# One group fewer by seven products, state's copy on ScalarE, and the y products in a portion of their own

## The chip, the cores and the metric

The kernel runs on one core of a Trainium2 chip. TensorE (PE) multiplies, VectorE (DVE), ScalarE (ACT) and GpSimd (POOL) do the element-wise work, and transfers are issued from queues, most of the weights' from SyncE's (SP). The metric is the device time of one execution in microseconds (us); before the change the median of three runs is 1458.86 us, from 1458.23 to 1462.82.

## What is computed

One decoder layer on 256 tokens of width 2048, in float32. A normalised input is multiplied by one wide matrix, whose columns are split into the gate z, the inputs x, B, C and dt of a state-space part (SSD), and q, k, v of an attention part:

```python
def hybrid_mixer(u, w_in, ...):
    z, xbc, dt_raw, q, k, v = jnp.split(u @ w_in, IN_SPLITS, axis=-1)
    xbc = silu(causal_depthwise_conv(xbc, conv_w, conv_b))
    xs, bm, cm = jnp.split(xbc, ...)          # 8 groups of 4 heads of 64
    y = ssd_chunked(xh, softplus(dt_raw + dt_bias), -exp(a_log), bm, cm) + d_skip * xh
    yg = y * silu(z)
    yg = yg * rsqrt(mean(yg * yg, axis=-1) + EPS)      # by group
    y_att = dilated_window_attention(...)              # three dilations, combined
    return concat([yg * ssm_norm_w, y_att]) @ w_out

h = x + rmsnorm(hybrid_mixer(rmsnorm(x), ...))
out = h + rmsnorm(relu(rmsnorm(h) @ w_up) ** 2 @ w_down)
```

`ssd_chunked` works on two chunks of 128 tokens. Inside a chunk y is (C Bᵀ, masked and multiplied by decays) times x·dt. The second chunk also gets C times the state that the first leaves, times a decay. That second term is `yo` below, and the first chunk's state is `st`.

## The kernel before

**Products.** The 256 tokens are two tiles of 128, the 2048 rows of a weight 16 tiles of 128. Weights come in blocks of two row tiles and 512 columns (`raw`, four buffers, SP's queue), and a block is one k step. Since TensorE multiplies in a reduced form of fp32, every tile is split in two: ScalarE rounds it to `hi` (line 147) and VectorE takes the rest, `lo` (line 148), with five buffers of each. The buffer of a `hi` is free again once TensorE has finished the block of five steps before. Each product is then hi·hi + hi·lo + lo·hi: three matmuls of 512 columns where tokens are the rows of the result (`row_tile`, lines 328 to 330). For x, B and C the features are the rows, and one matmul of 512 columns (line 475, the two parts of the tokens side by side) and one of 256 (line 478) do it.

**Seven products.** z, v, out, up and down are made in units of two column blocks (`unit`). `order` is the order of their k steps, and a group k that is named in `by_seven` is multiplied in Strassen's manner (`seven`): for two column blocks and two row tiles, seven products of three matmuls (lines 411 to 413) in place of eight. It pays for that with sums of weights (`pair`, added up by transfers on POOL's queue, and three adds on VectorE, line 252), with four weight tiles to split instead of two, and with sums of the tokens' blocks (`sums_of_acts`, lines 368 to 371 and a split), which are made once for each k and kept in `sums_of`. z has two units, at about 85 to 127 us and 235 to 277 us, and both use the same sums. At the first group by seven of a unit all waiting work is drained.

**Head groups.** `ssd_group` is a generator for one of the eight groups of four heads, and what lies between two of its `yield`s is a portion. After each conversion block of x two of them are appended to `waiting`, and `pump` runs one portion of each in turn as the k steps of the next products go by, so the instructions of a pair of groups stand interleaved with matmuls of x, B, C. The four pairs lie at about 128 to 162, 176 to 208, 279 to 311 and 320 to 346 us. A group's work in order: C·B and the transpose of B (lines 793, 794), which ScalarE copies to `bn` (799); transposes of x (804), copied to `xs` (806); x·dt on VectorE (809); on POOL `xdd` (811) and the skip term (813); the decays `bc` on ScalarE (820, 821; exp needs a table load when SiLU came before) and VectorE (822); the state's matmul (825) and copy (827); state times C (829), times decay `yo` (831), added by POOL (833); the y products (837), the gate and norm (840 to 855); the last transposes (857), split into `sh` (149) and `sl` (150) for the output product.

All these small results go through two banks of PSUM (`psm`, tiles named ps). A matmul into a ps tile waits until the engine that reads the tile before in that bank has done so. The order in which instructions stand on an engine is set by the scheduler from the program's order and its priorities; each engine runs its own in that order.

The conversion block (`conv`, lines 744 to 753) and the additions of the two halves of a feature product (`added`, lines 498 and 499) run beside it on the same engines.

Of the kernel before, what the change touches and what calls it, by code (L numbers as in the profile page):

```python
# [13 lines left out]
AF = mybir.ActivationFunctionType  # L14
# [3 lines left out]
S = 256  # L18
# [59 lines left out]
def hymba_layer(ctx: ExitStack, tc: tile.TileContext, x, norm_mix_pre, w_in, conv_w, conv_b, dt_bias, a_log,  # L78
                d_skip, ssm_norm_w, w_out, norm_mix_post, norm_mlp_pre, w_up, w_down, norm_mlp_post,
                consts, out):  # L80
    nc = tc.nc
# [53 lines left out]
    def psmall():  # L135
        return psm.tile([P, NB], F32, name="ps")

    def rsqrt_mean(dst, sums, n):

        m = cp.tile(list(sums.shape), F32, name="rm", bufs=2)  # L140
        nc.vector.tensor_scalar(m, sums, 1.0 / n, EPS, op0=ALU.mult, op1=ALU.add)
        nc.gpsimd.tensor_tensor(dst, m, half[:, :sums.shape[1]], op=ALU.pow)

    def split(hi, lo, src, scale=None):

        if scale is None:
            return (nc.scalar.activation(hi, src, AF.Copy),  # L147
                    nc.vector.tensor_tensor(lo, src, hi.bitcast(F32), op=ALU.subtract))  # L148
        return (nc.scalar.activation(hi, src, AF.Copy, scale=scale),
                nc.vector.scalar_tensor_tensor(lo, src, scale, hi.bitcast(F32), op0=ALU.mult, op1=ALU.subtract))  # L150
# [105 lines left out]
    w_z, w_v, w_ups, w_downs = w_in[:, COL_Z:], w_in[:, COL_V:], [w_up[:, hf * 4096:] for hf in range(2)], [w_down, w_down[4096:]]  # L256
    orders = {}

    def order_of(ks, by_seven):
        return [(k, k in by_seven) for k in ks]  # L260

    def plan(name, src, n, order, by_seven):

        orders[name, n] = order_of(order, by_seven)
        pairs.extend((src, n * NB, k) for k in order if k in by_seven)
# [157 lines left out]
            nc.vector.tensor_tensor(b[0], more[1], u, op=ALU.add)  # L423
            nc.vector.tensor_tensor(b[1], more[3], b[0], op=ALU.add)

    plan("z", w_z, 0, (0, 2, 4, 6, 1, 3, 5), (1, 3, 5))
    plan("z", w_z, 2, (0, 2, 1, 4, 3, 6, 5), (1, 3, 5))
    for n in (0, 2):
        plan("v", w_v, n, range(7), V_SEVENS)
# [353 lines left out]
    def ssd_group(sp, g, bT, cT, xT, z):  # L783

        hs = slice(HPG * g, HPG * (g + 1))
        bc = sp.tile([P, HPG, S], F32, name="bc")
        nc.scalar.dma_start(bc, acs_d[hs].partition_broadcast(P))
        yield

        p = psmall()  # L790
        for c in range(NT):
            cs = slice(c * P, (c + 1) * P)
            nc.tensor.matmul(p[:, cs], bT[:, cs], cT[:, cs], start=True, stop=True)
        nc.tensor.transpose(p[:, S:S + P], bT[:, 0:P], ident)
        cbm = sp.tile([P, NT, P], F32, name="cbm")
        nc.vector.tensor_tensor(cbm, p[:, :S].rearrange("p (c i) -> p c i", c=NT),
                                triu[:, None, :].to_broadcast([P, NT, P]), op=ALU.mult)
        bn = sp.tile([P, P], F32, name="bn")
        nc.scalar.activation(bn, p[:, S:S + P], AF.Copy)

        p = psmall().rearrange("p (c f) -> p c f", c=NT)
        for c in range(NT):
            for f in range(2):
                nc.tensor.transpose(p[:, c, f * P:(f + 1) * P], xT[:, f, c * P:(c + 1) * P], ident)
        xs = sp.tile([P, NT, HPG, HD], F32, name="xs")
        nc.scalar.activation(xs.rearrange("p c r d -> p c (r d)"), p, AF.Copy)
        xdt = sp.tile([P, NT, HPG, HD], F32, name="xdt")
        for c in range(NT):
            nc.vector.tensor_tensor(xdt[:, c], xs[:, c], dt[:, c, hs, None].to_broadcast([P, HPG, HD]), op=ALU.mult)
        xdd = sp.tile([P, HPG, HD], F32, name="xdd")  # L810
        nc.gpsimd.tensor_tensor(xdd, xdt[:, 0], toend[:, hs, None].to_broadcast([P, HPG, HD]), op=ALU.mult)
        for c in range(NT):
            nc.gpsimd.tensor_tensor(xs[:, c], xs[:, c], skip_b[:, hs, None].to_broadcast([P, HPG, HD]), op=ALU.mult)
        yield

        for c in range(NT):
            m = bc[:, :, c * P:(c + 1) * P]
            for r in range(HPG):
                h = HPG * g + r
                nc.scalar.activation(m[:, r], m[:, r], AF.Relu, scale=-1.0, bias=acs[:, c, h:h + 1])  # L820
            nc.scalar.activation(m, m, AF.Exp, scale=-1.0)
            nc.vector.tensor_tensor(m, m, cbm[:, c, None, :].to_broadcast([P, HPG, P]), op=ALU.mult)

        p = psmall()
        nc.tensor.matmul(p[:, :S], bn, xdd.rearrange("p r d -> p (r d)"), start=True, stop=True)
        st = sp.tile([P, HPG * HD], F32, name="st")
        nc.vector.tensor_copy(st, p[:, :S])
        yield
        nc.tensor.matmul(p[:, S:], cT[:, P:], st, start=True, stop=True)
        yo = sp.tile([P, HPG, HD], F32, name="yo")  # L830
        nc.vector.tensor_tensor(yo, p[:, S:].rearrange("p (r d) -> p r d", r=HPG),
                                eacs[:, hs, None].to_broadcast([P, HPG, HD]), op=ALU.mult)
        nc.gpsimd.tensor_tensor(xs[:, 1], xs[:, 1], yo, op=ALU.add)
        p = psmall().rearrange("p (c r d) -> p c r d", c=NT, r=HPG)
        for c in range(NT):
            for r in range(HPG):
                nc.tensor.matmul(p[:, c, r], bc[:, r, c * P:(c + 1) * P], xdt[:, c, r], start=True, stop=True)  # L837

        yg = sp.tile([P, NT, HPG * HD], F32, name="yg")
        nc.vector.tensor_tensor(yg, p.rearrange("p c r d -> p c (r d)"), xs.rearrange("p c r d -> p c (r d)"),  # L840
                                op=ALU.add)
        nc.vector.tensor_tensor(yg, yg, z, op=ALU.mult)
        gs = sp.tile([P, NT], F32, name="gs")
        for c in range(NT):
            junk = sp.tile([P, HPG * HD], BF16, name="gj")
            nc.scalar.activation(junk, yg[:, c], AF.Square, accum_out=gs[:, c:c + 1])
        gr = sp.tile([P, NT], F32, name="gr")
        rsqrt_mean(gr, gs, HPG * HD)
        for c in range(NT):
            nc.vector.tensor_scalar(yg[:, c], yg[:, c], gr[:, c:c + 1], None, op0=ALU.mult)  # L850
        yield
        yield
        yield
        p = psmall().rearrange("p (f s) -> p f s", f=2)
        for f in range(2):
            for c in range(NT):
                nc.tensor.transpose(p[:, f, c * P:(c + 1) * P], yg[:, c, f * P:(f + 1) * P], ident)
        with tc.high_priority(offset=200):
            for f in range(2):
                k = 2 * g + f  # L860
                split(sh[:, k], sl[:, k], p[:, f], w_ssm[:, k:k + 1])
# [3 lines left out]
    for hb in range(2):  # L865
        bT = conv_block(COL_B + hb * NB, 16 + 4 * hb, first if hb == 0 else None)
        if hb == 0:
            waiting.append(steps())
        cT = conv_block(COL_C + hb * NB, 24 + 4 * hb)
        for xb in (2 * hb, 2 * hb + 1):  # L870
            xT = conv_block(COL_X + xb * NB, 4 * xb)
            if xb % 2 == 0:
                zs += gates(xb)
            for j in range(2):
                g = 2 * xb + j
                waiting.append(ssd_group(sp, g, bT[:, g % 4], cT[:, g % 4], xT[:, 2 * j:2 * j + 2],
                                         zs[xb][:, :, j * 256:(j + 1) * 256]))
# [623 lines left out]
```

## Time and profile before

| | |
|---|---|
| median of 3 runs | 1458.86 us (1458.23 to 1462.82) |
| profiled execution | 1459.04 us |
| its span in the trace | 1457.3 us |
| granted TensorE clock, mean | 0.999 |
| TensorE busy | 1446.1 us |
| VectorE busy | 1281.2 us |
| ScalarE busy | 939.1 us |
| GpSimd busy | 150.3 us |
| largest queue of transfers | 272.37 MB, 58.6% of 16 engines' span |

The span is what the instructions' records cover; 1.7 us of the execution lie around it. Busy time is the union of an engine's instructions, which on TensorE overlap: a row's "mean ns" is the length of one matmul, not what the next waits. In a row of the timeline the first number is the start, the second how long the row (one instruction or several of a kind) lasts; out<-in are the tiles by their names in the program; a bracket at the end is the engine's idle time before it, with what ended it. Line numbers are those of the kernel before.

### The profile page before, as it was taken

The numbers are of one execution on the slowest core, as the hardware profiler recorded it, in microseconds if no ns is written. First come the engines' busy times: TensorE is split into PE (matmuls) and PEld (weight loads), VectorE is DVE, ScalarE is ACT, GpSimd is POOL, SyncE is SP. The second block draws the span as 40 slices with busy tenths as digits, with TensorE's granted clock in tenths as the row PEclk, the third lists the DMA queues.
The fourth block names the chain that finished last, engine by engine and source line by source line (L and its number), as shares of the span: only waits on it lengthen the run. The fifth ranks groups of instructions, "written<-read, shape, count | busy, mean of one in ns | idle before, by whom it ended". The sixth has DMA issues, their size and how long they took to land.

```text
span 1457.3 us, 20381 instructions
## 1 busy us (share of the span) xinstructions
PE 1446.1 (99%) x7099; PEld 1219.4 (84%) x7099; DVE 1281.2 (88%) x1843; ACT 939.1 (64%) x1346; POOL 150.3 (10%) x226
## 2 busy tenths in 40 slices
PE   9999999999999999999999999999999999999998
PEld 8888888888888888888888888888888888888886
DVE  7799898888997686689878999999889999999997
ACT  7577779566666565556657677656464776765664
POOL 0202120121010010010100011011111111101000
PEclk9999999999999999999999999999999999999999
DMA  8978556856675486688876798678888888788854
GB/s 271 279 204 235 177 175 185 247 174 202 186 220 174 130 238 202 194 261 253 270 224 213 207 318 240 196 223 255 249 238 275 257 245 247 208 281 258 260 181 160
DMA packets 170201, 328.27 MB, mean 225 GB/s; under 512 B 15617, under 2 KB 18545, under 8 KB 170097
## 3 DMA queue, kind: packets, MB, share of 16 engines
q1 hardware_dynamic: 144592, 272.37, 58.6%
q0 software_dynamic: 17632, 40.91, 14.0%
q10 hardware_dynamic: 7872, 13.68, 2.7%
q8 instruction: 56, 0.92, 0.2%
q14 instruction: 49, 0.39, 0.1%
HBM read 322.67 MB, written 45.12 MB: 252 GB/s over the span
## 4 chain that ended last, share of the span: by engine, by line
PE 95%; DVE 3%; ACT 1%; issue 1%; POOL 0%; ACTq 0%; DVEq 0%
PE acc L475 13%; PE acc L328 11%; PE acc L330 11%; PE acc L329 11%; PE acc L478 7%; PE acc L412 6%; PE acc L413 6%; PE acc L411 6%; PE ps L330 3%; PE ps L328 3%; PE ps L329 3%; PE ps L412 3%; PE ps L413 2%; PE ps L411 2%; DVE lo L148 1%; PE ps L837 1%
## 5 line engine op out<-in xcount | busy, mean ns | idle before, releaser
L148 DVE TENSOR_TENSOR lo<-raw,hi 128x1024 fp32r<-128x1024 f32 (+1 forms) x392 | 476.8, 1221 | 86.0 <-ACT hi L147 82.7
L147 ACT ACTIVATE hi<-raw 128x1024 fp32r<-128x1024 f32 (+1 forms) x392 | 409.7, 1050 | 209.0 <-PE acc L330 70.6
L475 PE MATMUL acc<-ua,hi 128*128 128x512 f32 x600 | 162.5, 400 | 0.0
L475 PEld LDWEIGHTS acc<-ua,hi 128*128 128x128 f32 x600 | 105.5, 189 | 16.4
L147 ACT ACTIVATE hi<-e 128x1024 fp32r<-128x1024 f32 x64 | 68.1, 1064 | 69.1 <-DVE e L252 64.2
L478 PEld LDWEIGHTS acc<-ua,lo 128*128 128x128 f32 x600 | 88.2, 190 | 10.0
L478 PE MATMUL acc<-ua,lo 128*128 128x256 f32 x600 | 91.5, 282 | 0.0
L328 PE MATMUL acc<-hi,sh 128*128 128x512 f32 x224 | 88.4, 395 | 0.0
L330 PE MATMUL acc<-hi,sl 128*128 128x512 f32 x224 | 87.3, 390 | 0.0
L329 PE MATMUL acc<-lo,sh 128*128 128x512 f32 x224 | 87.2, 389 | 0.0
L328 PE MATMUL acc<-hi,ua 128*128 128x512 f32 x216 | 85.5, 396 | 0.0
L329 PE MATMUL acc<-lo,ua 128*128 128x512 f32 x216 | 84.2, 390 | 0.0
L330 PE MATMUL acc<-hi,ua 128*128 128x512 f32 x216 | 84.2, 390 | 0.0
L148 DVE TENSOR_TENSOR lo<-e,hi 128x1024 fp32r<-128x1024 f32 x64 | 78.0, 1219 | 0.0
L475 PE MATMUL acc<-uc,hi 128*128 128x512 f32 x240 | 69.9, 402 | 0.0
L412 PE MATMUL acc<-lo,ah 128*128 128x512 f32 x174 | 67.8, 390 | 0.0
L411 PE MATMUL acc<-hi,ah 128*128 128x512 f32 x174 | 67.8, 389 | 0.0
L413 PE MATMUL acc<-hi,al 128*128 128x512 f32 x174 | 67.7, 389 | 0.0
L148 DVE TENSOR_TENSOR lo<-ha,hi 128x1024 fp32r<-128x1024 f32 x43 | 52.3, 1221 | 5.9 <-ACT hi L147 5.7
L147 ACT ACTIVATE hi<-ha 128x1024 fp32r<-128x1024 f32 x43 | 45.1, 1056 | 16.2 <-PE acc L330 9.5
L147 ACT ACTIVATE hi<-r 128x512 fp32r<-128x512 f32 x64 | 40.1, 627 | 18.3 <-PE acc L330 7.0
L330 PE MATMUL acc<-hi,al 128*128 128x512 f32 x128 | 49.8, 389 | 0.0
(544 smaller groups left out, 3612.7 us busy)
## 6 DMA issues: line engine op xcount, KB each, us to landing
raw<-in_w_in_dram SPq DMA_DIRECT2D x161, 512.0 KB, 4.5
raw<-in_w_down_dram SPq DMA_DIRECT2D x72, 512.0 KB, 5.2
raw<-in_w_up_dram SPq DMA_DIRECT2D x65, 512.0 KB, 4.7
raw<-in_w_out_dram SPq DMA_DIRECT2D x38, 512.0 KB, 5.1
pair<-in_w_up_dram POOLq DMA_DIRECT2D x56, 256.0 KB, 5.0
raw<-pair SPq DMA_DIRECT2D x52, 256.0 KB, 4.2
pair<-in_w_down_dram POOLq DMA_DIRECT2D x50, 256.0 KB, 6.2
ha<-in_w_up_dram SPq DMA_DIRECT2D x20, 512.0 KB, 4.9
```

Source lines behind the costliest of these rows:

```text
L147: return (nc.scalar.activation(hi, src, AF.Copy), nc.vector.tensor_tensor(lo, src, hi.bitcast(F32), op=ALU.subtract))
L148: nc.vector.tensor_tensor(lo, src, hi.bitcast(F32), op=ALU.subtract))
L328: nc.tensor.matmul(dst, a_h[:, r, ts], hi[:, j], start=begin and j == 0, stop=False)
L329: nc.tensor.matmul(dst, a_h[:, r, ts], lo[:, j], start=False, stop=False)
L330: product[t] = nc.tensor.matmul(dst, a_l[:, r, ts], hi[:, j], start=False, stop=end and j == KB - 1)
L411: nc.tensor.matmul(dst, a_h, hi[:, j], start=own and first, stop=False)
L412: nc.tensor.matmul(dst, a_h, lo[:, j], start=False, stop=False)
L413: nc.tensor.matmul(dst, a_l, hi[:, j], start=False, stop=own and last)
L475: nc.tensor.matmul(acc[f], hi[:, j, f * P:(f + 1) * P], u(k0 + j), start=k0 + j == 0, stop=False, skip_group_check=True)
L478: nc.tensor.matmul(acc[f][:, 0], lo[:, j, f * P:(f + 1) * P], u(k0 + j)[:, 0], start=False, stop=k0 + j == NK - 1, skip_group_check=True)
L837: nc.tensor.matmul(p[:, c, r], bc[:, r, c * P:(c + 1) * P], xdt[:, c, r], start=True, stop=True)
```

## The change

Three edits, all shown in the diff. First, in the first unit of z the group k = 5 leaves `by_seven` and is multiplied by eight ordinary products; in the second unit it stays. Its sums of the tokens' blocks, which the first unit made for both, are now made in the second. Second, the copy of the state out of PSUM goes from VectorE to ScalarE, once for each group. Third, a `yield` now stands ahead of the y products, and one of the three ahead of the last transposes is gone; the number of portions stays. From line 835 on the changed kernel's lines are one higher, until the removed one.

```diff
-    plan("z", w_z, 0, (0, 2, 4, 6, 1, 3, 5), (1, 3, 5))
+    plan("z", w_z, 0, (0, 2, 4, 6, 1, 3, 5), (1, 3))
...
         st = sp.tile([P, HPG * HD], F32, name="st")
-        nc.vector.tensor_copy(st, p[:, :S])
+        nc.scalar.activation(st, p[:, :S], AF.Copy)
         yield
...
         nc.gpsimd.tensor_tensor(xs[:, 1], xs[:, 1], yo, op=ALU.add)
+        yield
         p = psmall().rearrange("p (c r d) -> p c r d", c=NT, r=HPG)
...
             nc.vector.tensor_scalar(yg[:, c], yg[:, c], gr[:, c:c + 1], None, op0=ALU.mult)
-        yield
         yield
         yield
```

In instructions, TensorE has 3 more, VectorE 13 fewer, ScalarE 6 more, POOL 2 and SP 1 fewer. From about 360 us on every engine's order is what it was; before, the portions' instructions stand at other places. The three places that follow are those on which the prediction rests. Tiles have their running numbers here, which differ between the two programs.

On TensorE, first pair of groups, around state times C (L829) and the y products (L837), before; hi_1659 and lo_1660 are the last block of x's product, hi_1747 the first of the next:

```order
L829 MATMUL ps_1566<-st_1568,cT_760 128x256
L475 MATMUL acc_1392<-uc_78,hi_1659 128x512 x2
L478 MATMUL acc_1392<-uc_78,lo_1660 128x256 x2
L475 MATMUL acc_1393<-uc_78,hi_1659 128x512 x2
L478 MATMUL acc_1393<-uc_78,lo_1660 128x256 x2
L837 MATMUL ps_1634<-xdt_1481,bc_1418 128x64 x8
```

The same place in the changed kernel, from the second group's L829 on (the first group's stands one block earlier); the y products are L838 here:

```order
L829 MATMUL ps_1587<-st_1589,cT_760 128x256
L475 MATMUL acc_1678<-ua_76,hi_1684 128x512 x2
L478 MATMUL acc_1678<-ua_76,lo_1685 128x256 x2
L475 MATMUL acc_1679<-ua_76,hi_1684 128x512 x2
L478 MATMUL acc_1679<-ua_76,lo_1685 128x256 x2
L475 MATMUL acc_1680<-ua_76,hi_1684 128x512 x2
L478 MATMUL acc_1680<-ua_76,lo_1685 128x256 x2
L475 MATMUL acc_1681<-ua_76,hi_1684 128x512 x2
L478 MATMUL acc_1681<-ua_76,lo_1685 128x256 x2
L838 MATMUL ps_1704<-xdt_1464,bc_1401 128x64 x8
```

The y products of the first group came half a block after its L829, and now come two blocks after it.

On ScalarE, last pair, around the copies of B's transposes (`bn`, L799) of groups 6 and 7, before:

```order
L147 ACTIVATE hi_3623<-raw_3621 128x1024
L753 ACTIVATE cT_3217<-cT_3217,par_96 128x256
L749 ACTIVATE cT_3217<-pad_3239,cw_97 128x256
L799 ACTIVATE bn_3376<-ps_3370 128x128
L806 ACTIVATE xs_3383<-ps_3378 128x512
L820 ACTIVATE bc_3300<-bc_3300,acs_448 128x128 x4
L820 ACTIVATE bc_3324<-bc_3324,acs_448 128x128
L147 ACTIVATE hi_3645<-raw_3643 128x1024
L753 ACTIVATE cT_3217<-cT_3217,par_96 128x256
L799 ACTIVATE bn_3398<-ps_3392 128x128
```

And in the changed kernel:

```order
L147 ACTIVATE hi_3566<-raw_3564 128x1024
L821 ACT_TABLE_LOAD
L821 ACTIVATE bc_3289<-bc_3289 128x4x128
L753 ACT_TABLE_LOAD
L753 ACTIVATE cT_3160<-cT_3160,par_96 128x256
L147 ACTIVATE hi_3611<-raw_3609 128x1024
L799 ACTIVATE bn_3365<-ps_3359 128x128
L806 ACTIVATE xs_3372<-ps_3367 128x512
L820 ACTIVATE bc_3289<-bc_3289,acs_448 128x128 x3
L806 ACTIVATE xs_3394<-ps_3389 128x512
L147 ACTIVATE hi_3656<-raw_3654 128x1024
L149 ACTIVATE sh_79<-ps_3425,par_96 128x256
```

An exp and a SiLU, each with its table load, now stand ahead of group 6's bn, and a hi and an sh stand between group 7's xs and its bn (bn_3387, the row after the last).

On TensorE, last pair in the changed kernel, from group 7's C·B (L793) to the last transposes of groups 4 and 5 (L857):

```order
L475 MATMUL acc_3197<-uc_78,hi_3436 128x512 x2
L793 MATMUL ps_3381<-cT_2271,cT_1952 128x128 x2
L794 MATMUL ps_3381<-ident_84,cT_1952 128x128
L804 MATMUL ps_3389<-ident_84,cT_3160 128x128 x4
L475 MATMUL acc_3198<-uc_78,hi_3436 128x512 x2
L478 MATMUL acc_3195<-uc_78,lo_3437 128x256 x2
L857 MATMUL ps_3425<-ident_84,yg_3230 128x128 x4
L478 MATMUL acc_3196<-uc_78,lo_3437 128x256 x2
L478 MATMUL acc_3197<-uc_78,lo_3437 128x256 x2
L478 MATMUL acc_3198<-uc_78,lo_3437 128x256 x2
L475 MATMUL acc_3195<-uc_78,hi_3483 128x512 x2
L857 MATMUL ps_3456<-ident_84,yg_3253 128x128 x4
```

Before, group 7's L793 stood in the block ahead of this one, between its L475 rows. Now it is one block later, and both transposes L857 follow it closely.

## The prediction

> **What bounds the kernel now.** I read the totals, then the chain of waits, then the busy times by stretch of 20 us, then the list of TensorE's own waits, and only then the timelines around the edited lines. Totals and chain, from the page:
>
> ```profile
> PE 1446.1 (99%) x7099; PEld 1219.4 (84%) x7099; DVE 1281.2 (88%) x1843; ACT 939.1 (64%) x1346; POOL 150.3 (10%) x226
> PE 95%; DVE 3%; ACT 1%; issue 1%; POOL 0%; ACTq 0%; DVEq 0%
> ```
>
> TensorE (PE) is busy 1446.1 of 1457.3 us and carries 95% of the chain. The stretches that the edits touch (start and end; PE, weight loads, DVE, ACT and POOL busy; granted clock; DMA share; GB/s):
>
> ```profile
> 140.00:160.00 20.00, 19.27 (x121) 17.15 (x120) 17.47 (x28) 8.36 (x16) 6.50 (x8) 1.00 0.69 208
> 180.00:200.00 20.00, 18.07 (x106) 15.71 (x105) 20.00 (x35) 16.79 (x33) 5.97 (x8) 1.00 0.52 149
> 320.00:340.00 20.00, 19.51 (x120) 16.73 (x119) 19.13 (x34) 18.47 (x39) 4.64 (x6) 1.00 0.55 148
> ```
>
> The granted clock is 1.00, and PE loses 0.7, 1.9 and 0.5 us in them. A faster engine elsewhere is worth nothing unless it removes one of PE's own waits. All of these in the whole program (engine, line, what released it; total us, times, longest):
>
> ```profile
> PE ps L825 <- DVE sl L150: 1.8, 1, 1.8
> PE ps L1353 <- ACT dg L1352: 1.7, 1, 1.7
> PE ps L526 <- DVE half L515: 1.1, 1, 1.1
> PE ps L837 <- DVE yo L831: 0.7, 1, 0.7
> PE ps L793 <- ACT bn L799: 0.5, 1, 0.5
> PE acc L1131 <- DVE ha L1122: 0.2, 1, 0.2
> PE ps L412 <- DVE lo L148: 0.2, 1, 0.2
> PE ps L829 <- DVE st L827: 0.2, 1, 0.2
> ```
>
> They sum to 6.4 us. L1353, L526 and L1131 (3.0 us) lie in code that is the same before and after; the other five, 3.4 us, lie where the edits act. That is 0.23% of the time, so a large gain is excluded before anything is costed.
>
> What a matmul costs PE is its distance to the next, not the listed duration (0.39 for one of 512 columns), since they overlap. From the chain of waits, an undisturbed block of a feature product:
>
> ```profile
> 41.09 1.84 PE acc L475 x8
> 42.93 0.95 PE acc L478 x8
> ```
>
> So 0.23 us for 512 columns, 0.12 us for 256, and 2.8 us a block. Measured from starts, a wait comes out 0.15 to 0.3 us longer than the list has it, since PE also takes time to get going again.
>
> **Edit 1, group 5 of the first unit of z by eight products.** Seven products are 21 matmuls of 512 columns, eight are 24: 3 × 0.23 = **+0.68 us**, certain, because PE has no free time there to put them into. What goes with it is the wait in the third seven products:
>
> ```profile
> 115.10 0.39 PE L411 MATMUL acc<-hi,ub 128*128 128x512 f32 x1
> 115.66 0.50 PE L412 MATMUL ps<-lo,ub 128*128 128x512 f32 x1 [0.17 <-DVE lo L148]
> 116.00 0.39 PE L413 MATMUL ps<-hi,ub 128*128 128x512 f32 x1
> ```
>
> Starts are 0.56 and 0.34 apart where 0.23 is due: 0.33 + 0.11 = 0.44 us lost. The group that replaces it asks VectorE for no weight sums (three adds of 0.7 and two splits fewer), so the wait has nothing left to cause it: **−0.44**, bounds −0.44 to 0. The sums of the tokens' blocks for k = 5 are shared by both units and are now made in the second; some 2.4 us of VectorE's work moves there with the split's two operations on ScalarE. There VectorE waits for ScalarE itself:
>
> ```profile
> 257.38 2.59 DVE L148 TENSOR_TENSOR lo<-raw,hi 128x1024 fp32r<-128x1024 f32 x2 [1.23 <-ACT hi L147]
> ```
>
> and PE waits nowhere. I cost the move at 0; if that one idle piece were its only cover, 2.4 − 1.2 = 1.2 us would show, so 0 to +1.2. The queues lose one load (SP) and the two transfers of a pair sum (POOL); no PE wait is on a DMA, so 0. Edit 1: **+0.24**.
>
> **Edits 2 and 3, by pairs of head groups.** The generators of two groups run interleaved, one portion per k step, so the four pairs are four places. The y products go one portion later, the last transposes lose one of their empty portions, and state's copy leaves VectorE for ScalarE.
>
> *Pair 0, 1 (128 to 162 us).* PE, VectorE and ScalarE:
>
> ```profile
> 148.03 0.60 PE L829 MATMUL ps<-st,cT 128*128 128x256 f32 x2
> 149.64 0.40 PE L478 MATMUL acc<-uc,lo 128*128 128x256 f32 x2
> 150.76 2.00 PE L837 MATMUL ps<-xdt,bc 128*128 128x64 f32 x16 [0.73 <-DVE yo L831]
> 150.30 0.41 DVE L831 TENSOR_TENSOR yo<-ps,eacs 128x256 f32<-128x256 f32 x1
> 147.32 1.06 ACT L147 ACTIVATE hi<-raw 128x1024 fp32r<-128x1024 f32 x1 [2.16 <-PE acc L475]
> ```
>
> The y products need the bank that yo empties, and start at 150.76 where 149.64 + 2 × 0.12 = 149.88 was possible: 0.88 us. yo ended 2.7 us after the L829 of its group began; the order now puts two blocks and the second L829 between, some 6 us. So **−0.88**, bounds −0.88 to 0. State's copy now stands on ScalarE, at worst behind one hi of 1.06 us, while its reader L829 comes two blocks, 5.6 us, after L825: 0. ScalarE was busy for 8.4 of 20 us there, and the copy itself is a wash (a ScalarE copy of that size out of the same memory, and VectorE's of state):
>
> ```profile
> 330.17 0.38 ACT L498 ACTIVATE cT<-acc 128x256 f32<-128x256 f32 x1
> 198.16 0.42 DVE L827 COPY st<-ps 128x256 f32<-128x256 f32 x1
> ```
>
> *Pair 2, 3 (176 to 208 us).* The largest wait:
>
> ```profile
> 191.77 0.67 PE L825 MATMUL ps<-xdd,bn 128*128 128x256 f32 x2 [1.76 <-DVE sl L150]
> 198.63 0.70 PE L829 MATMUL ps<-st,cT 128*128 128x256 f32 x2 [0.17 <-DVE st L827]
> 187.28 1.63 DVE L148 TENSOR_TENSOR lo<-raw,hi 128x1024 fp32r<-128x1024 f32 x1
> 190.02 1.21 DVE L148 TENSOR_TENSOR lo<-raw,hi 128x1024 fp32r<-128x1024 f32 x1
> 191.15 0.86 DVE L150 SCALAR_TENSOR_TENSOR sl<-ps,par,sh 128x256 fp32r<-128x256 f32 x2
> 185.75 2.08 POOL L813 TENSOR_TENSOR xs<-xs,skip_b 128x256 f32<-128x256 f32 x2
> ```
>
> L825 of group 2 needs the bank of group 0's transposes, which the last sl of L150 empties at about 191.6; VectorE is 20.00 of 20 busy, so it is a backlog that an order of the same work can't clear. The moved copy is not in it (198.16, after the wait). In the new order the transposes and L825 stand at the same places, with a lo less ahead of one sl: I take **−0.45**, bounds −1.76 (it goes) to +0.3. L829's wait for VectorE's copy, 0.17 by its row and about 0.3 from starts, goes: **−0.30**. The lo at 187.28 took 1.63 us beside POOL's L813, against 1.21 at 190.02 without it. The Trainium skill, SBUF — State Buffer, "Who interferes with whom", gives this a cause: a VectorE instruction with two SBUF inputs contends with GpSimd instructions that read SBUF. By that rule, whatever takes POOL's L811 and L813 out of the backlog would also take wait away; the change leaves them behind xdt in the same portion, so the rule speaks for the wait staying.
>
> *Pair 4, 5 (279 to 311 us).* No row of the list lies there: 0.
>
> *Pair 6, 7 (320 to 346 us).* Here the order gets worse. ScalarE and PE before:
>
> ```profile
> 320.76 1.04 ACT L147 ACTIVATE hi<-raw 128x1024 fp32r<-128x1024 f32 x1
> 322.83 0.25 ACT L799 ACTIVATE bn<-ps 128x128 f32<-128x128 f32 x1
> 322.98 0.58 ACT L806 ACTIVATE xs<-ps 128x512 f32<-128x512 f32 x1
> 326.55 1.28 ACT L821 ACT_TABLE_LOAD   x1
> 327.84 0.63 ACT L821 ACTIVATE bc<-bc 128x512 f32<-128x512 f32 x1
> 329.33 0.46 ACT L149 ACTIVATE sh<-ps,par 128x256 fp32r<-128x256 f32 x1
> 320.32 0.61 PE L793 MATMUL ps<-cT 128*128 128x128 f32 x4
> 323.13 0.71 PE L793 MATMUL ps<-cT 128*128 128x128 f32 x4 [0.49 <-ACT bn L799]
> ```
>
> Group 7's L793 needs the bank that group 6's bn copy (L799) empties; it starts 2.81 us after group 6's, 0.49 late by its row and about 0.65 from starts. In the new order three waits replace this one, with t from the start of group 6's L793:
> (a) Ahead of bn on ScalarE now stand hi_3566, a table load, an exp, a table load, a SiLU piece and hi_3611: about 1.1 + 1.28 + 0.6 + 1.28 + 0.5 + 1.0, so bn ends near t = 5.9. PE arrives at 0.9 (nine small matmuls, at 0.61 for four that overlap) + 2.8 (a block) + 6 × 0.23 = 5.1: **0.8**.
> (b) Group 4's last transposes take the bank that group 7's xs copy empties, which follows bn, xs of group 6 (0.5) and three L820 (0.9): **0.35**.
> (c) Group 5's take the bank of group 7's bn_3387, and that stands on ScalarE behind hi_3656 and an sh. hi_3656 can't start until PE has left the block whose buffer it reuses, which ends only 0.46 us before these transposes. From there 1.05 + 0.36 + 0.26 = 1.67 us: **1.2**.
> With 0.5 for later, smaller waits (L829 of both groups, the state's copy now behind L820 and hi), the pair loses 2.85 in place of 0.65: **+2.2**, bounds −0.65 (nothing waits) to +5 (the rival below). Queued behind (c) on ScalarE are an exp and the conversions of the next C block; the hi after them waits for PE anyway.
> The rows show 1.28 us for a table load, with the exp starting 1.29 after it and no gap ahead. The Trainium skill, ScalarE: Activation LUTs, "What ACT_TABLE_LOAD costs", has about 1.28 us for the instruction but 2.7 with the drain; the two loads in (a) would then push bn by 2.8 us more and the whole to about 1462.5. The trace agrees with the shorter figure.
>
> **Sum:** +0.24 − 0.88 − 0.45 − 0.30 + 2.2 = +0.8 us on an execution of 1459.04 us (span 1457.3 and 1.7 around it), 0.18 above the median of 1458.86 of the three runs. I set the forecast at that median plus 0.8, **1459.7 us**: no change that can be told. About 0.3% (4.4 us) is what a measurement of this kernel can tell from no change; the runs before spread over 4.6 us.
>
> **Rivals.**
> 1. *The waits simply vanish.* All five go and no new one comes: +0.68 − 0.44 − 0.88 − 1.76 − 0.30 − 0.65 = −3.35, so 1455.5. For it: each wait is a single event, and a shift of a microsecond removes it. Against: VectorE is full from 180 to 200, and ScalarE, 18.47 of 20 from 320 to 340, gets more. A half of it, with the last pair no worse and only a part of the wait at 191 gone, is 0.24 − 0.88 − 0.75 = −1.4: 1457.5.
> 2. *ScalarE becomes the bound of the last pair, slower.* If its serial chain there (copies behind hi, hi behind PE's release of a buffer) stretches each of (a), (b) and (c) by a hi of 1.05, with one table load more on the way, that is 3 × 1.05 + 1.28 = 4.4 above my sum: 1464.1. It decides once ScalarE's work between the two L793 exceeds PE's 5.1 us by more than the 0.8 of (a). For it: only 1.5 us of 20 were free there. Against: each release by PE also waits, so the delays don't add fully; half of it is 1461.9.
> 3. *The backlog at 191 stays whole and the second unit of z shows 1.2.* 0.81 + 0.45 + 1.2 = +2.5: 1461.3.
>
> **Chances and range.** Forecast, 1458.5 to 1460.7: 0.40. Rival 1 in whole or half: 0.25. Rival 2: 0.22. Rival 3: 0.10. Something unseen: 0.03, either side. Range **1455.8 to 1463.3**; the likeliest case alone 1458.5 to 1460.7. Faster by over 0.3% needs below 1454.5, beyond even rival 1: 0.04. Slower by over 0.3% needs above 1463.3, the upper part of rival 2: 0.16. Within: 0.80.
>
> **What would show it.** In the list of PE's waits after: L412's row and the one of the y products on yo gone (edit 1, pair 0, 1); L825 on sl still there between 0.5 and 1.8; new rows on ScalarE's L799, for L793 and for L857, near 320 to 335 us, of 0.8 and 1.2; 24 matmuls of L328 to L330 more and 21 of L411 to L413 fewer around 115 us; stretches from 360 us on equal but shifted. A PE wait in the second unit of z, or L829 waiting for ScalarE's copy in the first pairs, would make a step wrong; all waits gone near 325 would make the forecast wrong toward rival 1.

## The result and the profile after

The changed kernel took 1455.62 us, median of 8 runs (1454.98 to 1456.94); the kernel before, run beside it, 1459.68 us (8 runs). The ratio is 0.997, 95% interval 0.996 to 0.9981: 2.8 to 5.8 us faster, about 4 by the medians. I had forecast 1459.7, no change, with 1455.8 as the low end of the range. The time is that of the first rival, all waits vanish (1455.5).

The profiled execution took 1456.18 us with a span of 1454.2, 3.1 us less than before. Totals and chain, from the page of the changed kernel:

```profile
PE 1445.8 (99%) x7102; PEld 1220.1 (84%) x7102; DVE 1274.4 (88%) x1830; ACT 939.2 (65%) x1352; POOL 149.4 (10%) x224
PE 98%; ACT 1%; DVE 1%; issue 0%; DVEq 0%; ACTq 0%
```

TensorE does three matmuls more and is busy as long as before; its share of the chain goes from 95 to 98%. What went is its waits. All that are left after the change (engine, line, what released it; total us, times, longest):

```profile
PE ps L1353 <- ACT dg L1352: 1.7, 1, 1.7
PE ps L526 <- DVE half L515: 1.1, 1, 1.1
PE ps L825 <- DVE sl L150: 0.6, 1, 0.6
PE acc L1131 <- DVE ha L1122: 0.2, 1, 0.2
PE ps L887 <- DVE mx L895: 0.2, 1, 0.2
```

L837 (L838 now) on yo, L793 on bn, L829 on st and L412 on lo are gone; L825 on sl has 0.6 of 1.8 us left; L887, in attention, is new and small. The same three stretches as in the prediction (start and end; busy PE, weight loads, DVE, ACT, POOL; clock; DMA share; GB/s):

```profile
140.00:160.00 20.00, 20.00 (x124) 17.82 (x122) 16.65 (x27) 10.31 (x17) 5.35 (x6) 1.00 0.55 158
180.00:200.00 20.00, 19.38 (x115) 16.98 (x113) 19.13 (x33) 15.26 (x27) 3.84 (x7) 1.00 0.47 136
320.00:340.00 20.00, 19.95 (x123) 17.40 (x122) 17.72 (x31) 17.27 (x36) 7.29 (x8) 1.00 0.52 140
```

PE was busy 19.27, 18.07 and 19.51 us there before. The last row is the last pair of groups, where I had expected the loss.

To say where the 3.1 us come from, I compared the starts of the same feature matmuls (L475, hi) in both traces, counted from the program's start, at the borders of stages: the 129th, 225th, 289th, 417th, 545th and 609th start at 59.79, 138.69, 167.44, 223.68, 317.53 and 349.08 us before. The table has, for the kernels of this study with that order of matmuls, how many us the stage got longer (+) or shorter (−) than before. What lies ahead of the 129th is left out: it differed by up to 2.3 us between profiles of kernels that are the same there. So is what lies behind the 609th, which differed by −0.4 to +0.7 us. For the changed kernel the two were 0.25 and 0.05 us longer, which is why its span is 3.1 us shorter and the stages 3.34. The stages themselves repeat: `only_yield`, the same program as `yield_timed` and run apart from it, differs from it by at most 0.02 us in each.

| kernel | z, first unit | pair 0, 1 | pair 2, 3 | second z, pair 4, 5 | pair 6, 7 | sum |
|---|---|---|---|---|---|---|
| my forecast | +0.24 | −0.88 | −0.75 | 0 | +2.2 | +0.8 |
| changed kernel | +0.13 | −0.99 | −1.76 | −0.26 | −0.45 | −3.34 |
| only_z (edit 1) | +0.13 | −0.72 | −0.01 | −0.01 | +0.01 | −0.60 |
| only_copy (edit 2) | +0.01 | −0.68 | +0.04 | −0.01 | +0.13 | −0.51 |
| z_copy (edits 1, 2) | +0.13 | −0.73 | +0.06 | 0.00 | +0.11 | −0.43 |
| yield_timed (edit 3) | 0.00 | −0.99 | −1.73 | −0.26 | −0.47 | −3.45 |
| copy_yield (edits 2, 3) | +0.01 | −0.99 | −1.74 | −0.26 | −0.45 | −3.44 |
| before_noskip | 0.00 | −0.72 | −1.35 | −0.01 | −0.13 | −2.21 |
| yield_noskip | +0.01 | −0.99 | −2.61 | −0.26 | −0.59 | −4.45 |
| yield_late_skip | 0.00 | −0.99 | −1.27 | −0.26 | −0.59 | −3.12 |
| copy_yield_late_skip | +0.01 | −0.99 | −2.61 | −0.26 | −0.42 | −4.28 |

### The profile page after: what moved, and what is told of

Read it like the earlier page. It is cut to its first block, busy times and chain, and to the rows that moved or that the text cites. A ratio compares the mean times of both kernels' runs of the same rounds, so it can differ in the third digit from the quotient of the medians.

```text
span 1454.2 us, 20373 instructions
## 1 busy us (share of the span) xinstructions
PE 1445.8 (99%) x7102; PEld 1220.1 (84%) x7102; DVE 1274.4 (88%) x1830; ACT 939.2 (65%) x1352; POOL 149.4 (10%) x224
## 4 chain that ended last, share of the span: by engine, by line
PE 98%; ACT 1%; DVE 1%; issue 0%; DVEq 0%; ACTq 0%
PE acc L475 15%; PE acc L328 11%; PE acc L330 11%; PE acc L329 11%; PE acc L478 7%; PE acc L412 6%; PE acc L411 6%; PE acc L413 6%; PE ps L330 3%; PE ps L329 3%; PE ps L328 3%; PE ps L411 3%; PE ps L412 3%; PE ps L413 3%; PE ps L838 1%; PE acc L1408 1%
## 5 line engine op out<-in xcount | busy, mean ns | idle before, releaser
L475 PE MATMUL acc<-ua,hi 128*128 128x512 f32 x600 | 164.0, 402 | 0.0
L475 PEld LDWEIGHTS acc<-ua,hi 128*128 128x128 f32 x600 | 105.6, 189 | 16.3
L478 PEld LDWEIGHTS acc<-ua,lo 128*128 128x128 f32 x600 | 88.2, 189 | 10.3
L478 PE MATMUL acc<-ua,lo 128*128 128x256 f32 x600 | 90.8, 281 | 0.0
L329 PE MATMUL acc<-lo,sh 128*128 128x512 f32 x224 | 87.2, 389 | 0.0
L329 PE MATMUL acc<-lo,ua 128*128 128x512 f32 x216 | 84.2, 390 | 0.0
L475 PE MATMUL acc<-uc,hi 128*128 128x512 f32 x240 | 69.5, 401 | 0.0
L412 PE MATMUL acc<-lo,ah 128*128 128x512 f32 x174 | 67.8, 389 | 0.0
```

The costliest lines, as they stand in the source:

```text
L329: nc.tensor.matmul(dst, a_h[:, r, ts], lo[:, j], start=False, stop=False)
L412: nc.tensor.matmul(dst, a_h, lo[:, j], start=False, stop=False)
L475: nc.tensor.matmul(acc[f], hi[:, j, f * P:(f + 1) * P], u(k0 + j), start=k0 + j == 0, stop=False, skip_group_check=True)
L478: nc.tensor.matmul(acc[f][:, 0], lo[:, j, f * P:(f + 1) * P], u(k0 + j)[:, 0], start=False, stop=k0 + j == NK - 1, skip_group_check=True)
```

## The experiments

**One edit at a time.** Edit 1 alone, `only_z`:

```diff
-    plan("z", w_z, 0, (0, 2, 4, 6, 1, 3, 5), (1, 3, 5))
+    plan("z", w_z, 0, (0, 2, 4, 6, 1, 3, 5), (1, 3))
```

> Only the first edit: group 5 of z's first unit by eight products. Theory (each wait belongs to one edit, and this one is worth nothing by itself): the wait of L412 for lo is gone, the first unit of z is 0.1 to 0.25 us longer than before (+0.68 for three matmuls, -0.44 for the wait), and PE's other four waits stay: L837 on yo near 0.7, L825 on sl near 1.8, L829 on st near 0.2, L793 on bn near 0.5. Span within 0.4 us of 1457.3. Rival (VectorE's or the queues' relief in z is what shortens the later waits): L825's wait falls by 0.5 us or more and the span is 1 us or more shorter.

One execution, 1459.46 us, span 1457.6. PE's waits between 128 and 350 us:

```profile
PE ps L825 <- DVE sl L150: 1.7, 1, 1.7
PE ps L793 <- ACT bn L799: 0.5, 1, 0.5
PE ps L829 <- DVE st L827: 0.2, 1, 0.2
```

As expected, L412's wait is gone, z is 0.13 longer and the two large waits stay. The rival falls: the wait on sl is as long as before. Not expected: L837's wait on yo is gone too, and that pair (0, 1) is 0.72 us shorter. Edit 1 also changes VectorE's order there: a product of the decays (L822) that stood at 147.10 us before, between state's copy and a lo, now comes ahead of 143.7 us, and yo comes in time. That this is the reason is read off the rows; no run moves that product alone.

Edit 2 alone, `only_copy`:

```diff
-        nc.vector.tensor_copy(st, p[:, :S])
+        nc.scalar.activation(st, p[:, :S], AF.Copy)
```

> Only the second edit: state's copy on ScalarE. Theory: L829's wait for st (0.17 by the list, 0.3 from starts) goes and nothing else does: L825 on sl 1.6 to 1.8, L837 on yo, L793 on bn and L412 stay; span 0.2 to 0.5 us shorter. Rival (the backlog of VectorE before L825 is shortened by the copies that leave it): L825 on sl at 1.2 or less and the span 0.8 us or more shorter.

One execution, 1460.25 us, span 1458.1 (its start-up was 1.34 us longer than before's by the 129th matmul). The wait on st is gone, and those on sl (1.7) and bn (0.5) stay. The list still has one on yo, of 0.4, but it is not the old one. That of pair 0, 1 is gone, which makes the pair 0.68 us shorter (two copies of state, of 0.41 us each, have left VectorE ahead of that yo), and a new one stands in pair 2, 3:

```profile
202.04 1.66 PE L837 MATMUL ps<-xdt,bc 128*128 128x64 f32 x13 [0.39 <-DVE yo L831]
```

Here only two of a block's L478 stand ahead of these y products, where before all eight did. So what the wait on st had cost is not saved: it comes back as a wait on yo, and the pair is 0.04 us longer. My expectation had the time about right (−0.51 us) and the place wrong. The rival falls: the copies that leave VectorE do nothing for L825.

Edit 3 alone, `only_yield`, and once more with timing, `yield_timed`:

```diff
         nc.gpsimd.tensor_tensor(xs[:, 1], xs[:, 1], yo, op=ALU.add)
+        yield
...
-        yield
         yield
         yield
```

> Only the third edit: the y products in a portion of their own. Theory: this edit does nearly all of it. L837 (L838 here) on yo is gone, L793 on bn is gone, L825 on sl falls to 0.5 to 0.9; L412 stays at 0.17 and L829 on st may stay at 0.2; span 2.5 to 3.2 us shorter than 1457.3. Rival (the three edits are needed together, the copy and the sums having to leave VectorE): L825 on sl stays above 1.3 and the span is less than 2 us shorter.

> The third edit alone again, timed. Theory (it does all of the change's work, the other two edits are worth nothing): ratio to before 0.996 to 0.998, like the changed kernel's 0.997. Rival (they add to it): 0.9985 or more.

One execution of the first: 1456.29 us, span 1454.2. PE's only wait between 128 and 350 us:

```profile
PE ps L825 <- DVE sl L150: 0.6, 1, 0.6
```

In these stages this is also all that the changed kernel has left; the wait on st went too, without moving the copy. L412's 0.2, in z, stays, as expected. Timed, the ratio to before is 0.9976 (0.9967 to 0.9985), beside 0.997 (0.996 to 0.9981) for all three edits. Stage by stage the third edit alone saves what the change saves, without the 0.13 us that edit 1 costs in z. The rival, that all three are needed, falls.

**Two at a time**, `z_copy` and `copy_yield`:

> The first and second edits without the third. Theory: the waits that need the third edit stay, L825 on sl 1.6 to 1.8 and L793 on bn 0.5; the small ones on lo, yo and st are gone or halved; span 0.3 to 1.0 us below 1457.3 at the same start. Rival: the two together shorten the wait on sl below 1.2.

> The second and third edits without the first. Theory (the first is worth nothing, the second only where VectorE's run ahead of the copy is long): the waits of the changed kernel (L825 on sl near 0.6) and L412's 0.17; pair by pair within 0.2 us of the third edit alone. Rival (the copy by itself saves L829's 0.3 us): pair 2, 3 saves 2.0 us or more against the 1.7 of the third edit alone.

Without the third edit the sum of the stages is −0.43 us (one execution, 1458.29), with L825 on sl at 1.7, L793 on bn at 0.5 and L837 on yo at 0.4, in pair 2, 3 again. With the second and third it is −3.44 (1456.50), that of the third alone to a few hundredths. The edits don't add: 1 and 2 each save in the first pair what 3 saves there anyway.

**The order inside a block turned round**, `lo_first`, from the changed kernel:

```diff
+        inner = 0 < k0 < NK - KB
+        for both in ((False, True) if inner else (True, False)):
             for f, j in order:
-                nc.tensor.matmul(acc[f], hi[:, j, f * P:(f + 1) * P], u(k0 + j), start=k0 + j == 0, stop=False,
...
-            for f, j in order:
-                nc.tensor.matmul(acc[f][:, 0], lo[:, j, f * P:(f + 1) * P], u(k0 + j)[:, 0], start=False,
...
+                if both:
+                    nc.tensor.matmul(acc[f], hi[:, j, f * P:(f + 1) * P], u(k0 + j), start=k0 + j == 0, stop=False,
...
+                else:
+                    nc.tensor.matmul(acc[f][:, 0], lo[:, j, f * P:(f + 1) * P], u(k0 + j)[:, 0], start=False,
```

> The changed kernel with the order inside a block of a feature product turned round (all k steps but the first and the last): the eight matmuls with lo first, then the eight with hi. Same work. Theory on what my prediction had wrong (a hi's buffer is free after the last matmul that reads hi, not at the end of the block): in the changed kernel the hi conversions start about 0.95 us before the block's end; here the last reader of hi is the end of the block, so ScalarE's conversions start 0.9 us later against the block, ScalarE waits longer for PE in feature products, and the waits that I had predicted for the pairs come up: PE's waits between 128 and 350 us sum to 1 us or more above the 0.8 of the changed kernel. Rival (the release was not what made the difference, there is slack on ScalarE anyway): PE's waits there within 0.4 us of the changed kernel's, span within 0.5 us of 1454.2.

One execution, 1458.07 us, span 1456.3. What ended ScalarE's waits ahead of a hi between 128 and 350 us, where it was a matmul of a feature product, in the changed kernel:

```profile
ACT hi L147 <- PE acc L475: 27.9, 19, 3.2
```

and with lo first, where three lines were added, so that line 478 is now the matmul with hi (and 481 that with lo):

```profile
ACT hi L147 <- PE acc L478: 12.5, 8, 4.0
```

In both it is the matmul that reads hi that frees the buffer, and never the one that reads lo; that part of the theory holds. The other part falls: the waits that I had predicted don't come back. PE's only wait in the pairs is 0.7 us, at 349 us, for the gated and normalised values of the last pair (yg), where the changed kernel has 0.6 on sl, and from the 225th to the 609th matmul with hi the pairs took 0.8 us less than in the changed kernel. The order of ScalarE's instructions had moved with the edit (no hi stands directly ahead of group 6's bn), so it isn't a test of one quantity. The rival's part, that the waits stay within 0.4 us of the changed kernel's, came true; its span did not. Of the 2.1 us by which the span is longer, 0.5 lie ahead of 60 us. The 0.8 us gained in the pairs are more than lost again by that wait at 349 us and one of 1.0 us at 402 us, where L329 waits for lo.

**Less work beside VectorE**, `before_noskip` and `yield_noskip`, from the kernel before and from the third edit alone:

```diff
-        for c in range(NT):
-            nc.gpsimd.tensor_tensor(xs[:, c], xs[:, c], skip_b[:, hs, None].to_broadcast([P, HPG, HD]), op=ALU.mult)
```

> The kernel before without POOL's two multiplications by the skip vector in each head group (line 813; the skip term stays unscaled, the result differs). The order on PE, VectorE and ScalarE is that of before; POOL has 16 instructions fewer. Theory (half of the largest wait, L825 on sl, was VectorE slowed by POOL beside it): x*dt (two) 1.25 to 0.75, the pads (two) 2.12 to 1.3 to 1.6, lo 1.63 to 1.22 us, 1.3 to 1.7 us in all, and the wait falls from 1.8 to 0.1 to 0.6 us; the other waits stay, but the yo wait of the first pair may fall by 0.4, the lo ahead of it having had 1.63 too. Span 1.3 to 2 us shorter than 1457.3. Rival (VectorE's run there is paced by ScalarE's hi and by PE, not by its own speed): the rows get shorter but the wait stays above 1.2.

> The third edit alone, without POOL's multiplications by the skip vector (the skip term stays unscaled). Theory: the last wait in the pairs, L825 on sl 0.6, goes (the pads 2.12 to about 1.3 and the decays' product 1.10 to about 0.7 us); no PE wait on sl, yo, st or bn is left and the span is 0.5 to 0.9 us below that of the third edit alone (1454.2). Rival: the wait stays above 0.4, the chain being ScalarE's.

Both leave out POOL's two multiplications by the skip vector in each group. One execution each, 1457.22 and 1454.83 us, spans 1455.2 and 1453.1. In the first, PE, VectorE and ScalarE run the same instructions in the same order as before, so only POOL's work differs. VectorE's rows ahead of L825 in `before_noskip` (start, length, line):

```profile
183.50 0.75 DVE L809 TENSOR_TENSOR xdt<-xs,dt 128x256 f32<-128x256 f32 x2
184.17 1.70 DVE L744 TENSOR_TENSOR pad<-cT,rbc 128x512 f32<-128x512 f32 x2
185.79 1.22 DVE L148 TENSOR_TENSOR lo<-raw,hi 128x1024 fp32r<-128x1024 f32 x1
```

The same rows in the kernel before:

```profile
184.07 1.25 DVE L809 TENSOR_TENSOR xdt<-xs,dt 128x256 f32<-128x256 f32 x2
185.24 2.12 DVE L744 TENSOR_TENSOR pad<-cT,rbc 128x512 f32<-128x512 f32 x2
187.28 1.63 DVE L148 TENSOR_TENSOR lo<-raw,hi 128x1024 fp32r<-128x1024 f32 x1
```

They are 0.50 + 0.42 + 0.41 = 1.33 us shorter, and L825's wait (L823 in this kernel) falls from 1.8 to 0.4:

```profile
PE ps L823 <- DVE sl L150: 0.4, 1, 0.4
```

The pair is 1.35 us shorter: what VectorE loses beside POOL is handed to TensorE whole. The first pair's wait on yo is gone with it, which I had expected to fall by 0.4 only. With the third edit the wait on sl is gone entirely. The rival, that ScalarE or PE sets the pace there, falls. The Trainium skill, SBUF — State Buffer, "Who interferes with whom", names the cause, a VectorE instruction with two SBUF inputs beside a GpSimd one that reads SBUF; all three kinds of row here are of that form, and the trace agrees. These rows took 1.25 to 1.7 times as long as without POOL's multiplications.

**The same work later**, `yield_late_skip`, from the third edit alone, and `copy_yield_late_skip`, the same edit on the second and third:

```diff
-        for c in range(NT):
-            nc.gpsimd.tensor_tensor(xs[:, c], xs[:, c], skip_b[:, hs, None].to_broadcast([P, HPG, HD]), op=ALU.mult)
...
+        nc.gpsimd.tensor_copy(xdd[:, 0, :HPG], skip_b[:, hs])
+        for c in range(NT):
+            nc.gpsimd.tensor_tensor(xs[:, c], xs[:, c], xdd[:, 0, :HPG, None].to_broadcast([P, HPG, HD]), op=ALU.mult)
         yield
         nc.tensor.matmul(p[:, S:], cT[:, P:], st, start=True, stop=True)
```

> The third edit alone, with POOL's multiplications by the skip vector held back until the state's matmul has read xdd (POOL copies the four skip values into xdd's buffer, and multiplies with them); the same result. The other engines' order is that of the third edit alone. Theory: as without them, no wait of L825 on sl; POOL's work falls beside other VectorE work that has time. Span 0.5 to 0.9 us below 1454.2; ratio to before 0.995 to 0.998. Rival: the contention only moves and yo's addition on POOL comes late, so that the y products or the gate wait: span at 1454.2 or above.

> The second and third edits with POOL's multiplications by the skip vector held back as before; z's first unit keeps its three groups. Theory (the contention moved on to the VectorE run ahead of state's copy, and ScalarE's copy is not in that run): no wait of PE on sl, yo, st or bn is left in the pairs; from the start of pair 2, 3 to its end 2.2 to 2.5 us are saved (1.7 with the third edit alone, 1.25 with the late skip and VectorE's copy), span 0.4 to 0.8 us below the third edit alone at the same start, 1453.2 to 1454.0; ratio to before 0.996 to 0.998. Rival: the wait moves once more, to yo or the gate, and the span is that of the third edit alone or above.

The first: median 1456.41 us, ratio 0.9977 (0.9968 to 0.9986). The wait on sl is gone as it should be, but a new one has come, and the pair saves 1.27 us in place of 1.73. The rival is right that the contention only moves, but the wait is for state's copy and not where it had put it, at the y products or the gate. PE, VectorE and POOL around it:

```profile
198.82 0.70 PE L830 MATMUL ps<-st,cT 128*128 128x256 f32 x2 [1.08 <-DVE st L825]
195.65 1.63 DVE L148 TENSOR_TENSOR lo<-raw,hi 128x1024 fp32r<-128x1024 f32 x1
198.35 0.41 DVE L825 COPY st<-ps 128x256 f32<-128x256 f32 x1
195.46 2.30 POOL L828 TENSOR_TENSOR xs<-xs,xdd 128x256 f32<-128x256 f32 x2
```

POOL's multiplications now meet the lo ahead of state's copy (1.63 us again), and state times C waits for that copy. So the second edit has a use after all: with the copy on ScalarE, in `copy_yield_late_skip`, no wait is left between 128 and 350 us, and pair 2, 3 is 2.61 us shorter, 0.85 more than in the changed kernel and a little over the 2.2 to 2.5 expected. The busy times of the stretch that had the largest wait:

```profile
180.00:200.00 20.00, 20.00 (x120) 17.76 (x119) 20.00 (x35) 15.89 (x31) 6.31 (x9) 1.00 0.54 156
```

VectorE is as full as before, 20.00 of 20, and PE no longer waits for it. The stages sum to −4.28 us against −3.34 for the change. Its median is 1455.60, ratio 0.9975 (0.9966 to 0.9984): by the clock it can't be told from the changed kernel (1455.62) or from the third edit alone (1455.97 us, 0.9976). Its profiled span is 1455.1, with a start-up 1.84 us longer than before's; with that of `only_yield`, 0.49, it would be 1453.75 beside 1454.2, as expected.

## Why the prediction was wrong

**The bound was right, and that the sum was met is in part luck.** TensorE's busy time hardly changed, and what went was its own waits. In the first rival's sum the five that lay in reach, less 0.68 us for the three added matmuls, were worth 3.35 us; the stages got 3.34 us shorter. The terms don't agree as the sums do: 0.6 us of the wait on sl stayed, while pair 4, 5 gave 0.26 us that no case had priced. Nor was 3.35 the most that could be had. In pair 2, 3, `yield_noskip` and `copy_yield_late_skip` save 2.61 us, where the first rival has 1.76 + 0.30 = 2.06; it took the 1.76 for L825 from the list, and from starts it is about 1.9. Edit 1 (+0.24 forecast, +0.13 measured) and the first pair (−0.88, −0.99) came as priced, though the first pair's wait was so loosely placed that any of the three edits removes most of it, as does taking POOL's multiplications out.

**The step that failed: "hi_3656 can't start until PE has left the block whose buffer it reuses".** The same belief put hi_3566 behind PE's earlier block in (a), where I counted its 1.1 us from the start of group 6's L793, and it stands in the description of the kernel, which has the buffer free once the block is finished. In these traces a hi's buffer is free when the last matmul that reads hi is done; after it a block still has its matmuls with lo, 0.95 us for eight. TensorE in the last pair of the changed kernel:

```profile
314.89 2.00 PE L475 MATMUL acc<-ua,hi 128*128 128x512 f32 x8
316.74 1.12 PE L478 MATMUL acc<-ua,lo 128*128 128x256 f32 x8
317.69 0.61 PE L793 MATMUL ps<-cT 128*128 128x128 f32 x4
322.92 0.71 PE L793 MATMUL ps<-cT 128*128 128x128 f32 x4
323.94 0.71 PE L475 MATMUL acc<-uc,hi 128*128 128x512 f32 x2
324.93 0.66 PE L857 MATMUL ps<-ident,yg 128*128 128x128 f32 x4
325.34 0.96 PE L478 MATMUL acc<-uc,lo 128*128 128x256 f32 x6
326.60 0.60 PE L857 MATMUL ps<-ident,yg 128*128 128x128 f32 x4
```

and ScalarE there (the rest of L753, xs of group 6, three L820 and an sh lie in between and are not shown):

```profile
316.93 1.06 ACT L147 ACTIVATE hi<-raw 128x1024 fp32r<-128x1024 f32 x1
318.01 1.28 ACT L821 ACT_TABLE_LOAD   x1
319.31 0.63 ACT L821 ACTIVATE bc<-bc 128x512 f32<-128x512 f32 x1
319.96 1.28 ACT L753 ACT_TABLE_LOAD   x1
321.67 1.04 ACT L147 ACTIVATE hi<-raw 128x1024 fp32r<-128x1024 f32 x1
322.62 0.25 ACT L799 ACTIVATE bn<-ps 128x128 f32<-128x128 f32 x1
324.28 0.60 ACT L806 ACTIVATE xs<-ps 128x512 f32<-128x512 f32 x1
324.77 1.05 ACT L147 ACTIVATE hi<-raw 128x1024 fp32r<-128x1024 f32 x1
326.07 0.28 ACT L799 ACTIVATE bn<-ps 128x128 f32<-128x128 f32 x1
```

- (a), forecast 0.8: the first hi starts at 316.93, as the eight matmuls with hi end (314.89 + 2.00), 0.76 us ahead of L793 and not behind it. Everything after it took what I had added up, so bn ends at 322.87, t = 5.18 in place of 5.9. PE comes at 322.92, t = 5.23 (forecast 5.1). It was a near thing, 0.05 us, and no wait.
- (b), forecast 0.35: xs of group 7 ends at 324.88 and the transposes start at 324.93. From starts they came some 0.2 us late.
- (c), forecast 1.2: the hi starts at 324.77, after the last matmul with hi (323.94 + 0.71) and 1.5 us ahead of the block's end (325.34 + 0.96 = 326.30). bn ends at 326.35, the transposes start at 326.60: 0.
- The 0.5 for later waits was not there either. The pair, forecast at +2.2, got 0.45 us shorter, by most of the 0.65 that waited before.

With the release at the block's end the same rows would have given what I forecast. In (a) bn would end 0.76 us later, at t = 5.94, 0.7 us behind PE. In (c) the hi could not start before 326.30, its bn would end 1.58 us later, at 327.88, and the transposes would come 1.3 us late. That is arithmetic on the rows: no run here delays the release and nothing else, since in `lo_first` ScalarE's order moved as well.

The trace of before had said so. In its list of what ended ScalarE's waits ahead of a hi between 128 and 350 us, fourteen of the fifteen that a feature product ended are put down to L475, the matmul with hi, and one to L478, at 282.20 us, which stays unexplained:

```profile
ACT hi L147 <- PE acc L475: 18.2, 14, 2.3
ACT hi L147 <- PE acc L478: 1.3, 1, 1.3
```

One of the fourteen is the row at 147.32 that the prediction shows. The rule of the Trainium skill that I had weighed, ScalarE: Activation LUTs, "What ACT_TABLE_LOAD costs", with 2.7 us including a drain, did not show: both loads took 1.28 us, and the exp started 1.30 after the first.

**The second miss, pair 2, 3: "it is a backlog that an order of the same work can't clear".** I forecast −0.75 and it was −1.76, of which 1.14 is the wait on sl. I had looked only at the stretch in which VectorE is full, not at when that stretch began. ScalarE and VectorE ahead of it in the kernel before:

```profile
176.16 1.28 ACT L821 ACT_TABLE_LOAD   x1
178.94 0.37 ACT L498 ACTIVATE cT<-acc 128x256 f32<-128x256 f32 x1
179.34 0.42 DVE L499 TENSOR_TENSOR cT<-acc,cT 128x256 f32<-128x256 f32 x1 [0.53 <-ACT cT L498]
183.42 0.60 PE L857 MATMUL ps<-ident,yg 128*128 128x128 f32 x4
```

and in the changed kernel:

```profile
169.94 1.28 ACT L821 ACT_TABLE_LOAD   x1
177.10 0.38 ACT L498 ACTIVATE cT<-acc 128x256 f32<-128x256 f32 x1
177.59 0.42 DVE L499 TENSOR_TENSOR cT<-acc,cT 128x256 f32<-128x256 f32 x1
189.37 0.86 DVE L150 SCALAR_TENSOR_TENSOR sl<-ps,par,sh 128x256 fp32r<-128x256 f32 x2
182.78 0.60 PE L857 MATMUL ps<-ident,yg 128*128 128x128 f32 x4
```

Before, VectorE stood idle for ScalarE's copy of the x block (L498), which stood behind a table load, an exp of the head groups and a hi; only then did its full run begin. With the third edit the table load and that exp come earlier, and the first of these additions (L499) starts 1.75 us sooner, 1.1 of it against the transposes L857 that PE does in the run (which are 0.64 earlier themselves). From there to the sl that L825 waits for it is as long as before, 11.81 us (191.15 − 179.34) and 11.78 (189.37 − 177.59), though the mix in it has changed (one lo fewer, two products of the decays more). So the 1.1 us by which it begins sooner is the 1.14 us by which the wait fell. The backlog was not cleared, it was begun earlier. That the third edit does it is shown by the kernels with one edit; that it does it by ScalarE's order is read off these rows, and no run changes that order alone.

And it was not all VectorE's own work: `before_noskip` shows 1.33 us of it to be POOL's. The prediction had named this contention, and drawn from it only that the wait would stay. The third edit also took the small wait for st, and 0.26 us in pair 4, 5, where the list of waits had no row but the starts showed two sets of y products 0.15 and 0.10 us late.

**The chances.** I gave the case that happened 0.25, because the last pair's forecast of +2.2 rested on an order whose chain I had added up correctly, from a wrong starting point. Without that term my sum would have been −1.4, and with the measured −1.76 for pair 2, 3 it would have been −2.4. The other 0.9 is 0.45 of the last pair's own wait, 0.26 in pair 4, 5, and 0.11 each in z and in the first pair. The range was also not in line with the chances: it began at 1455.8, above the 1455.5 of the first rival.

## What to carry to other kernels

When a wait is forecast from a buffer that must come free, ask which instruction reads it last, not when the step it belongs to ends; the releaser named in the list of waits tells it. A full engine is not yet a bound: see when its full run begins and what it was idle for just before. Where one engine slows another, moving the work can move the loss to whatever then stands next to it, so look at what waits there before moving it.

## What was not expected of the hardware

POOL's multiplications beside VectorE cost it 0.4 us in one lo of 1.2, in two different places (187.28 in the kernel before, 195.65 in `yield_late_skip`), and 1.33 us in one run of five instructions, all of which TensorE then waited. The time before 60 us, where the first inputs are loaded, differed by up to 2.3 us between profiles of kernels with the same instructions there, more than half of the whole effect, so that edits of this size had to be compared by stages.
